# Dealing the staged Strassen products evenly over the steps of an MLP, and starting four output gates before the last products are transposed

## The chip, the core and the metric

The kernel runs on one core of a Trainium2 chip. The metric is device time in microseconds of one execution. The median of three runs before the change is 1495.2 us (1494.3 to 1498.37). Lower is better.

## The reference

One decoder layer over 256 tokens of width 2048, in float32. Cut to what this change touches:

```python
r = r + merged @ w_o[i]                                        # attention and convolution branches, ahead of it
h = rms_norm(r, g_mlp[i])
r = r + jnp.square(jax.nn.relu(h @ w_up[i])) @ w_down[i]       # 2048 -> 8192 -> 2048
h = rms_norm(r, g_ple[i])
r = r + jax.nn.sigmoid(h @ w_ple_gate[i]) * (p[i] @ w_ple_proj[i])   # 2048 -> 2048, and 256 -> 2048
```

## The kernel before

Everything is held transposed: features on the 128 partitions, the 256 tokens along the row. A float32 number is split into a rounded high part and a low rest (`w_hi`/`w_lo`, and for activations the two halves of an `x` tile), and a product is built from high*high, high*low and low*high. ScalarE (ACT) makes the high part, VectorE (DVE) the low one. A **unit** is one 128-column slice of a weight matrix, 128x2048 numbers: `cols` runs 32 matmuls for it, 16 of 512 columns (weights high, both parts of the activation) and 16 of 256 columns (weights low). It writes one PSUM bank, `ps_up` for a slice of w_up, `ps_dn` for one of w_down, `ps_pg` for one of w_ple_gate.

The MLP is 96 **steps** g = 0..95, one unit each: four quarters, each of about 16 up units (`ps_up`) and then 8 down units (`ps_dn`). The down units cover output columns 8 to 15 of w_down (in slices of 128) for the 16 up results of their quarter. Output columns 0 to 7 are computed another way: seven products P1 to P7 (`P`, one PSUM bank each, Strassen's scheme on 2x2 blocks) accumulate over 32 pairs j of up results. Each pair goes through four **stages** x = 0..3, which load nothing new but make the high and low parts that the products read:

- x = 0: the sums `s_raw` of the up results, then `s` high and low, and `b_hi`/`b_lo` (B11 and B22);
- x = 1: `t` (T1 and T3), then `t_hi`/`t_lo`;
- x = 2: `t` (T2 and T4), and `b` high and low (B21);
- x = 3: `t_hi`/`t_lo` of these, and ahead of them the four `s_raw` sums of the next pair, if its up results are there.

The matmuls that belong to a stage (6, 6, 3 and 6 of 512 columns, `products`) stand one step later on TensorE, behind that step's unit. How many stages a step takes is a table worked out in front of the loop (`staged`, from `quota`).

From g = 2 on, each engine's instructions keep the order in which the program gives them (`ordered`). A step g gives: the load of unit g+3 (`load_raw`) and of the pair that is staged two steps later (`load_pair`); the unit's matmuls; the split of the first half of unit g+2 (`w_hi`, `w_lo`); the work on the results of the unit before (`up_sum`, `up_high`, `up_low`, or `dn_done`); the stages; the split of the second half of unit g+2; the copy of the unit's PSUM bank to SBUF on ACT (`evacuated`: tiles `up` or `dn`); the products. There is a single bank for the units of the MLP ([7], the other seven hold P1 to P7), so unit g+1 starts on TensorE only when ACT has copied unit g's bank, and that copy stands on ACT behind the stages and the second `w_hi` of its step. The `hi` and `lo` tiles are 7 each, shared by units and stages; the `raw` tiles that the loads fill are 4; other tiles of 2 KB a row come from 45 slots.

The residual waits in DRAM (`r_kept`). In the first three quarters `dn_done` adds a down result to it with two accumulating DMAs on the POOL queue, one for each half of the tile `dn`, into the same place. At g = 85 all eight 256-row pieces are loaded into tiles `r`. In the last quarter `dn_done` adds on DVE instead (`r<-dn`), and after every second unit calls `enter_ple`: the squares of the piece are added to `ss2` (`sq`, `ss`), and two `x` tiles (`hP`) are made for the output gates.

When the last stage's products have run, `end_products` combines P1 to P7 on DVE (`u2`, `c11`, `u3`, `c21`, `c12`, `c22`), and four groups of four 128x128 transposes (`tr`) bring the result into the layout of `r`, where DVE adds it (`end_r`, `r<-tr`) and `enter_ple` follows. Then sixteen output gates run (`ps_pg`, each with a small `ps_proj`); the first needs all sixteen `hP` tiles.

Of the kernel before, what the change touches and what calls it, by code (L numbers as in the profile page):

```python
# [8 lines left out]
F32 = mybir.dt.float32  # L9
# [7 lines left out]
P = 128  # L17
S = 256
# [18 lines left out]
def hybrid_block_kernel(ctx: ExitStack, tc: tile.TileContext, ins: dict, out: bass.AP):  # L37
# [18 lines left out]
    def slot(shape, dtype, name):  # L56
        return bp.tile(shape, dtype, tag="slot", name=name)
# [24 lines left out]
    def load(*args):  # L82
        return inorder(nc.sync.dma_start(*args))
# [392 lines left out]
    up_at = {i: g for g, (kind, i) in enumerate(units) if kind == "up"}  # L476
    NU = len(units)

    todo = [(j, x) for j in range(32) for x in range(4)]
    staged = []  # L480
    for g in range(NU + 1):
        kind = units[min(g, NU - 1)][0]
        quota = (2 if g >= 72 and g % 2 == 0 else 1) if kind == "up" else 3 if g >= 88 or g % 4 == 0 else 2
        some = []
        while todo and len(some) < quota and up_at[2 * todo[0][0] + 1] + 3 <= g:
            some.append(todo.pop(0))
        staged.append(some)
    assert not todo

    def stages(g):  # L490
        return staged[g] if 0 <= g < len(staged) else ()

    def load_raw(g):
        if g < NU:
            kind, i = units[g]
            w = ins["w_up"][i] if kind == "up" else ins["w_down"][16 * i[0] + i[1]]
            wU[g] = [wp.tile([P, UNIT], F32, tag="raw", name="raw", bufs=4)]
            load(wU[g][0], w)

    def half_tiles(name):  # L500
        return tuple(wp.tile([P, HALF], F32R, tag=t, name=f"{name}_{t}") for t in ("hi", "lo"))

    def unit_half(g, h):

        if g >= NU:
            return (lambda: None,) * 2
        raw = wU[g][0][:, h * HALF:(h + 1) * HALF]
        hi, lo = half_tiles("w")
        wU[g].append((hi, lo))
        return lambda: high(hi, raw), lambda: low(lo, raw, hi)  # L510
# [102 lines left out]
    def enter_ple(u):  # L613
        square_sum(ss2, len(hP), r[u])
        for i in range(2):
            xsplit(hP, 2 * u + i, r[u][:, i, :], col(G_PLE + 2 * u + i))

    def dn_done(q, n, st):
        if q < 3:
            for i in range(2):  # L620
                nc.gpsimd.dma_start(r_kept[n // 2][:, n % 2, :], st[:, i * S:(i + 1) * S], accum_op=ALU.add)
# [10 lines left out]
    def end_products():  # L632
# [11 lines left out]
        for n, m in ((0, (c11, c21)), (2, (c11, c21)), (4, (c12, c22)), (6, (c12, c22))):  # L644
            pending.append(lambda n=n, m=m: transposed(n, m, end_r))

    for g in range(2):
        load_raw(g)
        for h in range(2):
            for work in unit_half(g, h):  # L650
                work()
    load_raw(2)
    ended = False
    for g in range(NU):
        kind, i = units[g]
        ordered[0] = g > 1
        if g == 3:
            banks["acc"] = [7]
        load_raw(g + 3)
        for j, x in stages(g + 2):  # L660
            if x == 0:
                load_pair(j)
        if g == 85:
            for u in range(8):
                r[u] = slot([P, 2, S], F32, f"r_{u}")
                nc.gpsimd.dma_start(r[u], r_kept[u])
        xs = hT if kind == "up" else {k: uT[16 * i[0] + k] for k in range(16)}
        ps = cols(wU[g][1:], xs, f"{kind}_{g}")
        if g == 0:
            rstd1 = rstd_columns(ss1, "mlp")  # L670
        if g == 1:
            row1 = rstd_rows(rstd1, "mlp")
        done = [n for n in range(g) if n in evac] if g > 1 else []
        ups = [units[n][1] for n in done if units[n][0] == "up"]
        on_act, on_dve = unit_half(g + 2, 0)
        on_act()
        for n in done:
            if units[n][0] == "up":
                up_sum(units[n][1], evac.pop(n))
        on_dve()  # L680
        for k in ups:
            up_high(k)
        for k in ups:
            up_low(k)
        for n in done:
            if units[n][0] == "dn":
                dn_done(*units[n][1], evac.pop(n))
        for j, x in stages(g):
            for _, work in stage(j, x):
                work()  # L690
        for work in unit_half(g + 2, 1):
            work()
        evac[g] = evacuated(ps, kind)
        if kind == "up" and i == 63:
            up_sum(i, evac.pop(g))
            up_high(i)
            up_low(i)
        for j, x in stages(g - 1):
            products(j, x)
        if not ended and prod and not any(staged[g:]):  # L700
            ended = True
            end_products()
        run_pending(1)
    ordered[0] = False
    dn_done(3, 15, evac.pop(NU - 1))
    run_pending(len(pending))
    banks["acc"], banks["tr"] = [1, 2, 3, 4, 5, 7], [0, 6]


    praw = slot([P, 2, S], F32, "p")  # L710
# [19 lines left out]

    ready = []
    for n in range(16):
        wt = load_unit(ins["w_ple_gate"][n])
        if n % 4 == 0:
            wproj = load_half(ins["w_ple_proj"][n // 4])
        gate = cols(wt, hP, f"pg_{n}", flush=12)
        if n < 15:
            proj = cols([wproj], pT, f"proj_{n}", at=2 * (n % 4), nk=2)
        else:
            proj = bank("ps_proj_15")  # L740
            for k in range(2):
# [69 lines left out]
```

## Time and profile before

| | |
|---|---|
| median of three runs | 1495.2 us (1494.3 to 1498.37) |
| the profiled execution, its own time | 1497.43 us |
| its span, first to last instruction | 1495.7 us |
| TensorE busy (matmul / weight load) | 1452.7 us (97%) / 1239.2 us (83%) |
| VectorE, ScalarE, GpSimd busy | 1050.5 us (70%), 822.8 us (55%), 61.1 us (4%) |
| granted TensorE clock, mean | 0.992 |
| DMA | 288.89 MB, mean 193 GB/s |

Busy time of TensorE is that of modelled, overlapping matmuls, so 97% does not say that 97% of the span is at full pace: a matmul that runs at half clock is busy too. What an idle stretch of another engine costs is read from whether TensorE waits for it. Line 80 of the kernel is the helper that issues all matmuls, line 77 that of ACT, line 87 that of DVE, line 83 that of the loads, so the profile's rows are told apart by their tiles.

### The profile page before, as it was taken

Reading aid. Unit: us, or ns where it says so; the run is one execution under the profiler, and the core shown is the slowest. Engines: PE = TensorE matmul, PEld = TensorE weight load, DVE = VectorE, ACT = ScalarE, POOL = GpSimd, SP = SyncE. Lnnn points to the kernel's source line nnn. Section 1 sums busy time; section 2 is a strip of 40 time slices with the busy share of each in tenths; the row PEclk is TensorE's granted clock in tenths of the full one; section 3 lists DMA queues with packets and bytes.
Section 4 is the critical chain, followed back from the end, with each engine's and each line's share of the span. In section 5 each row is a group of like instructions: output and inputs, shape, how many; then the busy total and the mean of one; then the engine's idle time right before and its main releaser. Section 6 shows DMA issues by size and latency. Waiting matters only on the chain.

```text
span 1495.7 us, 19751 instructions
## 1 busy us (share of the span) xinstructions
PE 1452.7 (97%) x7528; PEld 1239.2 (83%) x7528; DVE 1050.5 (70%) x1547; ACT 822.8 (55%) x1280; POOL 61.1 (4%) x91
## 2 busy tenths in 40 slices
PE   8999999999999999999999999999999999988998
PEld 7888888888888888888887888788887878766887
DVE  7555677746455557668887688777887778876875
ACT  7655555454444445446665566555665556644543
POOL 0100000000000000000011000110001101000000
PEclk9999999999999999999999999999999999998999
DMA  9655445555655566554668565776557847544461
GB/s 340 223 171 189 172 173 169 179 194 190 197 192 189 185 250 205 205 182 169 217 188 233 180 206 188 199 209 193 215 169 199 252 157 258 165 151 155 161 216 39
DMA packets 133902, 288.89 MB, mean 193 GB/s; under 512 B 7600, under 2 KB 81584, under 8 KB 111792
## 3 DMA queue, kind: packets, MB, share of 16 engines
q1 hardware_dynamic: 125472, 277.11, 54.9%
q0 software_dynamic: 8192, 10.49, 4.2%
q8 instruction: 59, 0.97, 0.3%
q14 instruction: 35, 0.29, 0.1%
q10 hardware_dynamic: 144, 0.04, 0.0%
HBM read 277.12 MB, written 10.49 MB: 192 GB/s over the span
## 4 chain that ended last, share of the span: by engine, by line
PE 93%; DVE 2%; ACT 2%; issue 1%; DMA 1%; SPq 0%; ACTq 0%; DVEq 0%
PE ps_up L80 23%; PE ps_g L80 12%; PE ps_dn L80 11%; PE ps_conv L80 9%; PE P L80 9%; PE ps_o L80 6%; PE ps_y L80 6%; PE ps_pg L80 6%; PE ps_q L80 3%; PE ps_k L80 3%; PE ps_v L80 3%; ACT w_hi L77 1%; PE ps_proj L80 1%; DMA raw<-in_w_down_dram 1%; DVE t L87 1%
## 5 line engine op out<-in xcount | busy, mean ns | idle before, releaser
L87 DVE TENSOR_TENSOR w_lo<-raw,w_hi 128x1024 fp32r<-128x1024 f32 (+1 forms) x556 | 559.2, 1023 | 273.9 <-ACT w_hi L77 178.3
L77 ACT ACTIVATE w_hi<-raw 128x1024 fp32r<-128x1024 f32 (+1 forms) x556 | 486.4, 893 | 274.2 <-PE ps_g L80 66.7
L80 PE MATMUL ps_up<-x,w_hi 128*128 128x512 f32 x1024 | 257.8, 394 | 8.5 <-ACT up L77 8.5
L80 PEld LDWEIGHTS ps_up<-x,w_hi 128*128 128x128 f32 x1024 | 191.9, 189 | 52.9 <-ACT up L77 16.1
L80 PE MATMUL ps_g<-w_hi,x 128*128 128x512 f32 x512 | 159.1, 390 | 0.0
L80 PE MATMUL ps_dn<-x,w_hi 128*128 128x512 f32 x512 | 137.9, 415 | 19.8 <-ACT dn L77 19.8
L80 PEld LDWEIGHTS ps_dn<-x,w_hi 128*128 128x128 f32 x512 | 101.6, 201 | 45.8 <-ACT dn L77 25.4
L80 PEld LDWEIGHTS ps_up<-x,w_lo 128*128 128x128 f32 x1024 | 131.3, 191 | 5.0
L80 PE MATMUL ps_up<-x,w_lo 128*128 128x256 f32 x1024 | 132.8, 283 | 0.0
L77 ACT ACTIVATE t_hi<-t 128x1024 fp32r<-128x1024 f32 x64 | 67.6, 1056 | 109.9 <-DVE t L87 102.3
L80 PEld LDWEIGHTS ps_g<-w_hi,x 128*128 128x128 f32 x512 | 96.1, 188 | 19.8
L87 DVE TENSOR_TENSOR t_lo<-t,t_hi 128x1024 fp32r<-128x1024 f32 x64 | 78.3, 1223 | 44.8 <-ACT t_hi L77 31.3
L77 ACT ACTIVATE up<-ps_up 128x512 f32<-128x512 f32 x64 | 38.1, 595 | 119.2 <-PE ps_up L80 116.2
L80 PE MATMUL ps_g<-w_lo,x 128*128 128x512 f32 x256 | 99.6, 389 | 0.0
L80 PE MATMUL ps_conv<-x,w_hi 128*128 128x512 f32 x384 | 97.6, 397 | 0.0
L80 PEld LDWEIGHTS ps_conv<-x,w_hi 128*128 128x128 f32 x384 | 70.8, 188 | 13.3
L80 PE MATMUL ps_y<-w_hi,x 128*128 128x512 f32 x256 | 79.5, 389 | 0.0
L80 PE MATMUL P<-t_hi,s 128*128 128x512 f32 x192 | 70.2, 393 | 0.0
L80 PEld LDWEIGHTS ps_dn<-x,w_lo 128*128 128x128 f32 x512 | 65.6, 191 | 2.5
L80 PE MATMUL ps_dn<-x,w_lo 128*128 128x256 f32 x512 | 66.4, 283 | 0.0
L80 PE MATMUL ps_pg<-x,w_hi 128*128 128x512 f32 x256 | 64.7, 393 | 1.7 <-DVE x L87 1.7
L87 DVE TENSOR_TENSOR a<-up 128x256 f32<-128x256 f32 x64 | 27.1, 423 | 51.6 <-ACT up L77 51.6
(196 smaller groups left out, 2064.5 us busy)
## 6 DMA issues: line engine op xcount, KB each, us to landing
raw<-in_w_up_dram SPq DMA_DIRECT2D x64, 1024.0 KB, 5.1
raw<-in_w_in_dram SPq DMA_DIRECT2D x56, 1024.0 KB, 5.0
raw_s<-in_w_down_dram SPq DMA_DIRECT2D x128, 256.0 KB, 4.4
raw<-in_w_down_dram SPq DMA_DIRECT2D x32, 1024.0 KB, 5.4
raw<-in_w_qkv_dram SPq DMA_DIRECT2D x20, 1024.0 KB, 4.9
raw<-in_w_branch_dram SPq DMA_DIRECT2D x16, 1024.0 KB, 5.1
raw<-in_w_o_dram SPq DMA_DIRECT2D x16, 1024.0 KB, 4.9
raw<-in_w_ple_gate_dram SPq DMA_DIRECT2D x16, 1024.0 KB, 5.1
```

The source lines that it names most:

```text
L77: return inorder(nc.scalar.activation(*args, **kw))
L80: return inorder(nc.tensor.matmul(*args, **kw))
L87: return lambda *args, **kw: inorder(getattr(nc.vector, name)(*args, **kw))
```

## The change

**The table of stages.** Before, a down step takes 2 stages, every fourth one 3, and from step 88 on 3; an up step takes 1, and from step 72 on every second one 2. Now every down step takes 2, and an up step 1, and from step 76 on every second one 2. Stages per step:

| steps | before | now |
|---|---|---|
| 17 to 24 (down) | 2 2 2 3 2 2 2 3 | 2 2 2 2 2 2 2 2 |
| 25 to 28 (up) | 1 0 0 1 | 1 1 1 1 |
| 41 to 48, 49 to 52 | the same as 17 to 28 | the same as 17 to 28 |
| 65 to 72 (down) | 2 2 2 3 2 2 2 3 | 2 2 2 2 2 2 2 2 |
| 73 to 76 (up) | 1 0 0 2 | 1 1 1 2 |
| 77 to 87 (up) | 1 2 1 2 1 2 1 2 1 2 1 | the same |
| 88 to 95 (down) | 3 3 3 3 2 0 0 0 | 2 2 2 2 2 2 2 0 |

The last products so stand behind the unit of step 95, no longer of step 93. On DVE, in the last quarter, a step of before that takes three stages (x = 0, 1, 2 of a pair; `w_lo x2` is the second half of one unit and the first of the next):

```order
L87 TENSOR_TENSOR w_lo<-raw,w_hi 128x1024 x2
L87 TENSOR_TENSOR r_11340<-dn,r_11340 128x256 x2
L87 SCALAR_TENSOR_TENSOR x<-r_11340,vec,x 128x256 x2
L87 TENSOR_TENSOR b_lo<-raw_s,b_hi 128x1024
L87 TENSOR_TENSOR s_11791<-s_raw,s_11790 128x512
L87 TENSOR_TENSOR t_11796<-raw_s 128x1024
L87 TENSOR_TENSOR t_lo<-t_11796,t_hi 128x1024
L87 TENSOR_TENSOR t_11802<-raw_s,t_11796 128x512
L87 TENSOR_TENSOR t_11802<-t_11802,raw_s 128x512
L87 TENSOR_TENSOR b_1_11804<-raw_s,b_0_11803 128x512
```

and the step that takes the same pair's x = 0 and 1 now:

```order
L87 TENSOR_TENSOR w_lo<-raw,w_hi 128x1024 x2
L87 TENSOR_TENSOR b_lo<-raw_s,b_hi 128x1024
L87 TENSOR_TENSOR s_11833<-s_raw,s_11832 128x512
L87 TENSOR_TENSOR t_11838<-raw_s 128x1024
L87 TENSOR_TENSOR t_lo<-t_11838,t_hi 128x1024
```

The three instructions of x = 2 have moved to the next step, and the residual's additions and `x` tiles have left this one.

**The residual in the last quarter.** `dn_done` adds on DVE only for n = 12 to 15; n = 8 to 11 go to `r_kept` by accumulating DMAs, as in the quarters before. The pieces 0 to 3, 6 and 7 are loaded at g = 85, piece 4 at 92, piece 5 at 94, and `enter_ple` runs for piece 4 in step 94, 5 and 6 in step 95, 7 in step 96. The end of the POOL queue, before:

```order
L666 DMA r_11340<-r_kept_4627 128x512
L666 DMA r_11342<-r_kept_4628 128x512
L666 DMA r_11344<-r_kept_4629 128x512
L666 DMA r_11346<-r_kept_4630 128x512
L113 TENSOR_TENSOR rstd_ple<-rstd_ple,half 128x2
```

and now:

```order
L670 DMA r_11342<-r_kept_4630 128x512
L644 DMA r_kept_4627<-dn 128x256 x4
L644 DMA r_kept_4628<-dn 128x256 x2
L670 DMA r_11861<-r_kept_4627 128x512
L644 DMA r_kept_4628<-dn 128x256 x2
L670 DMA r_12010<-r_kept_4628 128x512
L113 TENSOR_TENSOR rstd_ple<-rstd_ple,half 128x2
```

Eight accumulations were put in, and the loads of pieces 4 and 5 stand behind those that they depend on.

**Halves of gates.** Two more steps, 96 and 97, take the second halves (k = 8 to 15) of the weights of gates 0, 1 and 2, 3. Their matmuls run into the banks of P2, P6, P4 and P5 once these are read; the first halves (k = 0 to 7) follow behind the loop, into the same banks. TensorE behind the last products, before (gate tiles are those of `ps_pg`; 12069 to 12208 are the four groups of transposes):

```order
L406 MATMUL tr_12069<-ident,c_12057 128x128
L406 MATMUL tr_12130<-ident,c_12057 128x128
L406 MATMUL tr_12069<-ident,c_12060 128x128
L406 MATMUL tr_12069<-ident,c_12057 128x128
L406 MATMUL tr_12069<-ident,c_12060 128x128
L80 MATMUL ps_dn_12084<-x,w_hi 128x512 x15
L80 MATMUL ps_dn_12084<-x,w_lo 128x256 x16
L80 MATMUL ps_dn_12084<-x,w_hi 128x512
L406 MATMUL tr_12130<-ident,c_12060 128x128
L406 MATMUL tr_12130<-ident,c_12057 128x128
L406 MATMUL tr_12130<-ident,c_12060 128x128
L80 MATMUL ps_dn_12145<-x,w_hi 128x512 x15
```

and now (12200, 12217, 12249 and 12266 are gates 0 to 3):

```order
L406 MATMUL tr_12174<-ident,c_12165 128x128
L406 MATMUL tr_12174<-ident,c_12162 128x128
L406 MATMUL tr_12174<-ident,c_12165 128x128
L80 MATMUL ps_pg_12200<-x,w_hi 128x512 x6
L406 MATMUL tr_12234<-ident,c_12165 128x128
L406 MATMUL tr_12234<-ident,c_12162 128x128
L406 MATMUL tr_12234<-ident,c_12165 128x128
L80 MATMUL ps_pg_12249<-x,w_hi 128x512 x6
L406 MATMUL tr_12283<-ident,c_12164 128x128
L406 MATMUL tr_12283<-ident,c_12166 128x128
L406 MATMUL tr_12283<-ident,c_12164 128x128
L406 MATMUL tr_12283<-ident,c_12166 128x128
```

The two down units between the transposes are gone from there, and six matmuls of gate 0 and six of gate 2 stand in their places; the rest of the four halves (gate 0: 10, gate 1: 16, gate 2: 10, gate 3: 16 matmuls) stands between the third and the fourth group of transposes.

The diff, cut to its core:

```diff
+    units += [("pg", (0, 1)), ("pg", (2, 3))]
+    gates = {}
...
-        quota = (2 if g >= 72 and g % 2 == 0 else 1) if kind == "up" else 3 if g >= 88 or g % 4 == 0 else 2
+        quota = 2 if kind == "dn" or g >= 76 and g % 2 == 0 else 1
...
+    def load_halves(raw, gates, h):
+        for i, n in enumerate(gates):
+            load(raw[:, i * HALF:(i + 1) * HALF], ins["w_ple_gate"][n][:, h * HALF:(h + 1) * HALF])
+
+    def gate_part(n, wt, ks, first):
+        ps = gates[n]
+        def high_part(k):
+            mm(ps, wt[0][:, k % 8 * P:(k % 8 + 1) * P], hP[k].rearrange("p a s -> p (a s)"), start=first and k == ks[0], stop=not first and k == ks[-1])
+        for k in ks if first else ks[:-1]:
+            high_part(k)
+        for k in ks:
+            mm(ps[:, S:], wt[1][:, k % 8 * P:(k % 8 + 1) * P], hP[k][:, 0, :], start=False, stop=False)
+        if not first:
+            high_part(ks[-1])
...
     def dn_done(q, n, st):
-        if q < 3:
+        if q < 3 or n < 12:
...
         else:
             add_to_r(n, st)
-            if n % 2 == 1:
-                enter_ple(n // 2)
...
         if g == 85:
-            for u in range(8):
-                r[u] = slot([P, 2, S], F32, f"r_{u}")
-                nc.gpsimd.dma_start(r[u], r_kept[u])
+            for u in (0, 1, 2, 3, 6, 7):
+                load_r(u)
+        if g in (92, 94):
+            load_r(g // 2 - 42)
+        if kind == "pg":
+            banks["acc"] = [1, 5, 3, 4] if i[0] == 0 else [3, 4, 2, 7]
...
+        for u in {94: (4,), 95: (5, 6), 96: (7,)}.get(g, ()):
+            enter_ple(u)
+        if kind == "pg":
+            for n, wt in zip(i, wU[g][1:]):
+                gates[n] = bank(f"ps_pg_{n}")
+                gate_part(n, wt, range(8, 16), True)
...
-    banks["acc"], banks["tr"] = [1, 2, 3, 4, 5, 7], [0, 6]
+    banks["acc"] = [2, 7, 1, 5, 3, 4]
...
-        gate = cols(wt, hP, f"pg_{n}", flush=12)
+        if n < 4:
+            gate = gates[n]
+            gate_part(n, split_half(raw[:, n % 2 * HALF:(n % 2 + 1) * HALF]), range(8), False)
+        else:
+            gate = cols(wt, hP, f"pg_{n}")
```

More of the change, by code (lines that the diff above doesn't have):

```diff
@@ L491, in stages @@
         return staged[g] if 0 <= g < len(staged) else ()
+    def load_halves(raw, gates, h):
[11 more added lines that the diff above has]
+            high_part(ks[-1])
     def load_raw(g):
-        if g < NU:
+        if g < len(units):
             kind, i = units[g]
-            w = ins["w_up"][i] if kind == "up" else ins["w_down"][16 * i[0] + i[1]]
             wU[g] = [wp.tile([P, UNIT], F32, tag="raw", name="raw", bufs=4)]
-            load(wU[g][0], w)
+            if kind == "pg":
+                load_halves(wU[g][0], i, 1)
+            else:
+                load(wU[g][0], ins["w_up"][i] if kind == "up" else ins["w_down"][16 * i[0] + i[1]])
     def half_tiles(name):
@@ L503, in unit_half @@
     def unit_half(g, h):
-        if g >= NU:
+        if g >= len(units):
             return (lambda: None,) * 2
@@ L645, in end_products, with load_r @@
             pending.append(lambda n=n, m=m: transposed(n, m, end_r))
+    def load_r(u):
+        r[u] = slot([P, 2, S], F32, f"r_{u}")
+        nc.gpsimd.dma_start(r[u], r_kept[u])
     for g in range(2):
@@ L653, in hybrid_block_kernel @@
     ended = False
-    for g in range(NU):
+    for g in range(len(units)):
         kind, i = units[g]
@@ L663, in hybrid_block_kernel @@
         if g == 85:
-            for u in range(8):
-                r[u] = slot([P, 2, S], F32, f"r_{u}")
-                nc.gpsimd.dma_start(r[u], r_kept[u])
-        xs = hT if kind == "up" else {k: uT[16 * i[0] + k] for k in range(16)}
-        ps = cols(wU[g][1:], xs, f"{kind}_{g}")
+            for u in (0, 1, 2, 3, 6, 7):
[4 more added lines that the diff above has]
+            banks["acc"] = [1, 5, 3, 4] if i[0] == 0 else [3, 4, 2, 7]
+        else:
+            xs = hT if kind == "up" else {k: uT[16 * i[0] + k] for k in range(16)}
+            ps = cols(wU[g][1:], xs, f"{kind}_{g}")
         if g == 0:
@@ L687, in hybrid_block_kernel @@
                 dn_done(*units[n][1], evac.pop(n))
+        for u in {94: (4,), 95: (5, 6), 96: (7,)}.get(g, ()):
+            enter_ple(u)
+        if kind == "pg":
+            for n, wt in zip(i, wU[g][1:]):
+                gates[n] = bank(f"ps_pg_{n}")
+                gate_part(n, wt, range(8, 16), True)
         for j, x in stages(g):
@@ L692, in hybrid_block_kernel @@
             work()
-        evac[g] = evacuated(ps, kind)
+        if kind != "pg":
+            evac[g] = evacuated(ps, kind)
         if kind == "up" and i == 63:
@@ L704, in hybrid_block_kernel @@
     ordered[0] = False
-    dn_done(3, 15, evac.pop(NU - 1))
     run_pending(len(pending))
-    banks["acc"], banks["tr"] = [1, 2, 3, 4, 5, 7], [0, 6]
+    banks["acc"] = [2, 7, 1, 5, 3, 4]
     praw = slot([P, 2, S], F32, "p")
@@ L732, in hybrid_block_kernel @@
     for n in range(16):
-        wt = load_unit(ins["w_ple_gate"][n])
+        if n >= 4:
+            wt = load_unit(ins["w_ple_gate"][n])
+        elif n % 2 == 0:
+            raw = wp.tile([P, UNIT], F32, tag="raw", name="raw", bufs=4)
+            load_halves(raw, (n, n + 1), 0)
         if n % 4 == 0:
             wproj = load_half(ins["w_ple_proj"][n // 4])
-        gate = cols(wt, hP, f"pg_{n}", flush=12)
+        if n < 4:
+            gate = gates[n]
+            gate_part(n, split_half(raw[:, n % 2 * HALF:(n % 2 + 1) * HALF]), range(8), False)
+        else:
+            gate = cols(wt, hP, f"pg_{n}")
         if n < 15:
```

## The prediction

> **What bounds the kernel now.** I read the page's busy times first, then who waits for whom on TensorE, then the busy times by stage, and last the chain of waits and the instructions in order of time inside the stages that lose time.
>
> ```profile
> span 1495.7 us, 19751 instructions
> PE 1452.7 (97%) x7528; PEld 1239.2 (83%) x7528; DVE 1050.5 (70%) x1547; ACT 822.8 (55%) x1280; POOL 61.1 (4%) x91
> ...
> PE ps_dn L80 <- ACT dn L77: 19.8, 8, 3.4
> PE ps_up L80 <- ACT up L77: 8.5, 10, 3.0
> ```
>
> TensorE is the bound, and its longest waits, 28.3 us, are for ACT's copy of the one bank of the MLP's units. The change removes no matmul, so it can only win back waits and their clock. The busy times by stretch show where these are (quarters 1 to 3 from the first down unit to the fourth up unit behind them, in the third to the fifth; the up steps 78 to 87; the down units 88 to 93; from there to gate 4):
>
> ```profile
> core 0: us, PE busy (x) PEld busy (x) DVE busy (x) ACT busy (x) POOL busy (x), PEclk, DMA share, GB/s
> ...
> 758.30:859.68 101.38, 97.53 (x523) 83.38 (x522) 77.36 (x101) 57.22 (x74) 13.67 (x16) 1.00 0.72 207
> 936.06:1038.98 102.92, 99.08 (x523) 84.54 (x522) 77.36 (x101) 57.21 (x74) 13.68 (x16) 0.98 0.71 204
> 1115.35:1224.71 109.36, 103.18 (x535) 87.83 (x534) 82.41 (x108) 60.29 (x80) 13.65 (x16) 0.97 0.71 205
> 1224.71:1299.63 74.92, 74.22 (x400) 63.61 (x399) 63.84 (x95) 46.84 (x66) 4.40 (x8) 1.00 0.63 206
> 1299.63:1367.09 67.46, 55.04 (x263) 45.36 (x262) 49.49 (x70) 32.66 (x43) 0.00 (x0) 0.92 0.47 158
> 1367.09:1415.74 48.65, 44.45 (x244) 37.39 (x244) 39.68 (x70) 27.95 (x49) 0.72 (x1) 0.96 0.47 162
> ```
>
> What these would take without a wait follows from the chain of waits, where it runs along TensorE undisturbed, and around step 44, where it leaves it:
>
> ```profile
> 936.06 5.55 PE ps_dn L80 x32
> ...
> 956.14 2.74 PE P L80 x12
> 958.88 3.67 PE ps_dn L80 x18
> ...
> 963.33 1.23 DVE b_lo L87
> 964.55 0.60 DVE s L87
> 965.15 1.15 DVE t L87
> ...
> 967.37 1.04 ACT w_hi L77
> 968.40 0.49 ACT dn L77
> ...
> 968.94 7.43 PE ps_dn L80 x32
> ```
>
> A unit takes 5.55 us, a product matmul 2.74 / 12 = 0.228. At g = 44 a third stage puts b_lo, s and t in front of ACT's `t_hi`, `w_hi` and copy; TensorE's own work (5.55 + nine products, 2.06) ends at 966.49, it starts again at 968.94, and then runs the unit in 7.43 us, at a lowered clock. Each stretch of the table, less this work (the table's counts have one or two matmuls that only cross its ends):
>
> - quarters 1 and 2: 13 units and 105 products, 96.1 us; lost 5.3 and 6.8
> - quarter 3: 13 units and 117 products, 98.8; lost 10.5
> - steps 78 to 87: 10 units and 78 products, 73.3; lost 1.6
> - down units 88 to 93: 6 units and 69 products, 49.0; lost 18.4.
>
> That is 42.6 us, and the tail's loss comes below.
>
> **The change part by part. Durations on DVE,** from step 76 (x = 0 and 1 beside an up result; the last row is TensorE's next unit in the chain of waits):
>
> ```profile
> 1208.07 0.29 DVE L87 TENSOR_TENSOR s_raw<-a 128x128 f32<-128x128 f32 x1
> ...
> 1209.00 1.22 DVE L87 TENSOR_TENSOR b_lo<-raw_s,b_hi 128x1024 fp32r<-128x1024 f32 x1
> 1210.13 0.69 DVE L87 TENSOR_TENSOR s<-s_raw,s 128x512 fp32r<-128x512 f32 x1
> 1210.73 1.22 DVE L87 TENSOR_TENSOR t<-raw_s 128x1024 f32<-128x1024 f32 x1
> 1213.08 1.23 DVE L87 TENSOR_TENSOR t_lo<-t,t_hi 128x1024 fp32r<-128x1024 f32 x1 [1.12 <-ACT t_hi L77]
> ...
> 1214.53 7.45 PE ps_up L80 x32
> ```
>
> From start to start DVE takes 1.13 us for 1024 columns, 0.6 for 512 and 0.93 for the four s_raw; these are the durations used throughout.
>
> **Quarters 1 to 3.** Steps with two stages already stand there: the one at 936.06 and the two behind it ran without a gap, with 5.55 us a unit and 6, 9 and 12 products between them. All eight down steps now have 9 or 12 products behind them (6 behind the first). ACT's second `w_hi` and copy take 1.04 + 0.49 behind a unit's end, under the 2.06 that nine products cover. DVE's work in the longer of the two kinds of step (x = 1 and 2) is two w_lo, t and t_lo at 1.13 us from start to start, three of 512 columns at 0.6, and the wait of 1.1 to 1.2 us for `t_hi`: 7.5 us, beside 8.3 us of TensorE (5.55 + 12 products). I count 0.1 to 0.2 us for eight such steps. The two empty up steps, in which no product covers the copy (8.5 us of such waits in 10), get 6 and 3 products; 3 products are 0.69 us, about the copy's time, for 0.2 to 0.3. So quarters 1 and 2 fall to 96.5 us each, from 101.4 and 102.9: **-4.9 and -6.4**. In quarter 3 step 76 stays tight, the one ahead of 1214.53. TensorE waited 3.0 there (the longest `up` wait above) and lost 7.45 - 5.55 = 1.9 on the clock behind it. Now six products stand in that wait (1.37), and the four s_raw are made a step earlier, in the stage x = 3 that has moved to step 75. That leaves 3.0 - 1.4 - 0.9, about 0.7 to 1, and I count no lowered clock behind it. Loss 1.6 in all, 100.4 us: **-9.0**.
>
> **The last quarter's down units.** Eight units and 69 products ahead of the last nine are 44.4 + 15.7 = 60.1 us. The stages stand in the other phase here (x = 2, 3 in one step, 0, 1 in the next). The dearer one, x = 0 and 1, costs DVE two w_lo, b_lo, t and t_lo at 1.13, s at 0.6 and the 1.2 us for `t_hi`: 7.4 us, beside 7.6 of TensorE; its partner 6.2 beside 8.3. For n = 8 to 11 the two additions (0.88 us a unit) leave DVE; for n = 12 to 14 they remain and meet step 93, which I count at 8.2 against 7.6. I take 1.5 us of loss for all eight, nearer to the quiet steps of the quarters before (0.1 each) than to the three-stage ones of this quarter (18.4 / 6 = 3.1 each), since no step has a third stage. 61.6 us from 1299.63.
>
> The eight accumulations go to POOL, whose queue is one behind the other (the last row is a weight load in the first quarter, the slowest that the chain of waits has there):
>
> ```profile
> POOL r_kept L621 <- DMA r_kept<-dn: 108.0, 24, 8.6
> ...
> r_kept<-dn POOLq DMA_DIRECT2D x48, 128.0 KB, 3.9
> ...
> r<-r_kept POOLq DMA_DIRECT2D x8, 256.0 KB, 6.0
> ...
> 768.69 0.85 POOL L621 DMA_DIRECT2D r_kept<-dn  x1 [2.97 <-DMA r_kept<-dn]
> ...
> 780.48 8.79 DMA raw<-in_w_down_dram
> ```
>
> A pair takes 108.0 / 24 + 0.85 = 5.35 us from its first issue to its second on the mean and 9.5 at worst, beside a step of 8. Piece 5's load then starts 10 us behind the copy of unit 91 (5.35, then 3.9 to landing, and the issue) and lands 6 us later, two steps on; ACT wants it one step after that, in step 95. I cost it at nothing, with one step as cover; were the pairs at their worst, it would come up to 6 us late. SP issues eight half loads of gates for four whole ones, four more issues; its queue waits on free tiles through all these steps.
>
> **The tail.** Before, from the end of unit 93 (1367.09) to gate 4:
>
> ```profile
> 1361.98 0.88 DVE L87 TENSOR_TENSOR r<-dn,r 128x256 f32<-128x256 f32 x2
> ...
> 1368.57 0.69 DVE L87 TENSOR_TENSOR u<-P,p 128x512 f32<-128x512 f32 x1 [1.36 <-PE P L80]
> ...
> 1373.90 0.69 DVE L87 TENSOR_TENSOR r<-tr,r 128x512 f32<-128x512 f32 x1
> ...
> 1376.90 0.61 ACT L77 ACTIVATE sq<-r 128x512 f32<-128x512 f32 x1
> 1377.42 0.89 ACT L77 ACTIVATE x<-r,vec 128x256 fp32r<-128x256 f32 x2
> ...
> 1379.97 0.33 PE tr L406 x3
> ...
> 1397.89 0.70 PE ps_proj L80 x4
> 1398.59 0.79 PE ps_ss_ple L80 x8
> ...
> 1404.17 0.43 PE ps_rstd_ple L80 x2
> ```
>
> Its work is nine products 2.05, two down units 11.1, sixteen transposes 1.7, four gates 22.2, four proj 2.8, ss and rstd 1.2: 41.1 of 48.65 us; it lost 7.6. Now the two down units stand ahead of it, and 30.0 us of work remain. Counted from the end of unit 95: one w_lo stands ahead of u on DVE, so u starts at 2.15, c21 ends at 5.8 (u, c11, u3 at 0.6, a w_lo 1.13, c21), the other three combinations at 7.6, the first r<-tr at 8.2, a w_lo at 9.3, then ss and two x for piece 0 (10.7), the last dn added (11.5), ACT's square and x (1.1) and DVE's two x: 13.4. Until then TensorE can do the products, twelve transposes (1.3) and the twelve gate matmuls that stand between them (2.6), 6.0 us; the rest of the halves stands behind gate 0's k = 14, which needs that x. So 7.4 us are lost, then 24.0 of work remain. With 1.1 for a lowered clock (once 1.7 or not at all) and for the first proj, which needs the load of p: **38.5 us**, lower end 30.0, upper end 42 (two lowered clocks, 3.4).
>
> **The sum.** Before 101.4 + 102.9 + 109.4 + 74.9 + 67.5 + 48.65 = 504.7. Now 96.5 + 96.5 + 100.4 + 74.9 + 61.6 + 38.5 = 468.4. Difference 36.3. The profiled execution took 1497.4 (span 1495.7) and lies 0.15% above the median of 1495.2; 1495.2 - 36.3 = **1459 us**. Nearly all of it comes from the table of stages; the tail loses as much as before.
>
> [...] The gap of 2.45 us ahead of 968.94 was followed by a unit at a lowered clock, 7.43 us for 5.55. [...]
>
> **The rivals.** (a) *Two stages are still too many in the last quarter.* For it: its step x = 0, 1 has 0.2 us of room, and w_hi waits for free tiles. Against it: the same seven tiles serve the quiet steps. Four such steps with the gap and clock of g = 44 (2.46 + 1.9) make 17 us less gain: 1476. (b) *The halves cover the tail.* If gate 0's k = 14 came by the time TensorE reaches it, the tail were 33 us and the time 1453; against it, the chain of DVE above has no slack. (c) *Slower: the accumulations hold up the end.* Piece 5 is queued behind eight accumulations and ACT behind piece 5 (its squares stand ahead of the last copies). It decides from where a pair takes so long that the 36 us are gone: four pairs, 6 us late at 9.5 each, so 9.5 + 30/4, about 17 us a pair, three times the mean: 1500 or more. [...] (d) *The deal changes nothing, since another wait ends last at the same time* (the raw loads: the 8.79 us of the row above are more than a step). Then quarters 1 to 3 keep their loss, 1479.
>
> **How the numbers follow.** The forecast (1450 to 1468) has 0.66, (a) or (d) in part or whole (1468 to 1482) 0.18, (b) 0.08, (c) 0.03; 0.05 is left for a wait that I don't see, half of it within 0.3% and half slower. A measurement here can tell about 0.3% (4.5 us) from no change. The hard floor is all the loss gone: 42.6 + 7.6, 1445. The range 1449 to 1476 leaves out (c), the end of (a) and (d), and the floor. Faster 0.66 + 0.18 + 0.08 = 0.92, same 0.03, slower 0.05.
>
> **What would show it.** Right: ACT's copies of `dn` no longer make TensorE wait in steps 17 to 24 and their like; the first three quarters' stretches at 96 to 101 us; the granted clock at 1.00 in them; down units 88 to 95 in 60 to 63; one wait of the transposes for c and one of `ps_pg` for x at the tail. Wrong: waits of ps_dn for ACT in the last quarter (a); ACT's `sq` waiting for r<-r_kept (c).

## The result, and the profile after

The changed kernel takes 1460.92 us (median of four runs, 1460.54 to 1460.98), beside 1496.5 for the kernel before on the same chip: ratio 0.9762, 95% interval 0.9745 to 0.9779. The forecast was 1459, in a range of 1449 to 1476. The profiled execution took 1460.54 us, with a span of 1458.7.

The head of the page, and the list of who makes TensorE wait (in total, how often, the longest), after:

```profile
span 1458.7 us, 19769 instructions
PE 1439.8 (99%) x7528; PEld 1232.5 (84%) x7528; DVE 1046.6 (72%) x1539; ACT 823.4 (56%) x1280; POOL 68.1 (5%) x99
...
PE tr L406 <- DVE c L87: 3.1, 2, 1.7
PE ps_up L80 <- ACT up L77: 2.8, 4, 1.1
PE ps_pg L80 <- DVE x L87: 1.9, 1, 1.9
PE ps_dn L80 <- ACT dn L77: 0.6, 1, 0.6
```

The two waits for ACT's copy were 19.8 and 8.5 us and are 0.6 and 2.8. DVE and ACT are as busy as before: no work went away, it only stands elsewhere. The busy times by stretch, cut at the same places as before, with the tail in the last row (length, then the busy times of PE, PEld, DVE, ACT and POOL, the granted clock, the DMA share, GB/s):

```profile
757.53:854.12 96.59, 96.59 (x522) 83.59 (x521) 77.87 (x102) 57.51 (x74) 13.75 (x16) 1.00 0.76 217
930.52:1027.11 96.59, 96.59 (x522) 83.60 (x521) 77.86 (x102) 57.62 (x74) 13.63 (x16) 1.00 0.76 217
1103.50:1204.27 100.77, 99.65 (x534) 85.77 (x533) 82.40 (x108) 60.32 (x80) 13.61 (x16) 1.00 0.76 215
1204.27:1278.76 74.49, 74.23 (x400) 63.62 (x398) 63.88 (x94) 47.00 (x66) 3.32 (x6) 1.00 0.62 211
1278.76:1340.15 61.39, 60.83 (x326) 52.09 (x325) 52.05 (x72) 38.13 (x51) 8.04 (x10) 1.00 0.76 223
1340.15:1378.90 38.75, 33.42 (x180) 27.66 (x179) 32.49 (x56) 22.22 (x41) 0.72 (x1) 0.96 0.47 170
```

In quarters 1 and 2 TensorE is busy for the whole of the stretch, at full clock. The chain of waits there, at the place of step 44, where it had left TensorE for DVE and ACT, is now unit, products, unit, with nothing between:

```profile
953.50 5.55 PE ps_dn L80 x32
959.05 2.06 PE P L80 x9
961.11 5.59 PE ps_dn L80 x32
```

The tail, from the end of unit 95 (1340.15) on, TensorE first, and then the splits (w_lo) that stand on DVE among the sums and x tiles (start, duration, and in brackets the idle time ahead and who ended it):

```profile
1344.04 0.30 PE L406 MATMUL tr<-ident,c 128*128 128x128 f32 x1 [1.66 <-DVE c L87]
...
1346.27 0.55 PE L406 MATMUL tr<-ident,c 128*128 128x128 f32 x3 [1.40 <-DVE c L87]
1346.57 2.51 PE L80 MATMUL ps_pg<-x,w_hi 128*128 128x512 f32 x6
...
1353.83 0.90 PE L80 MATMUL ps_pg<-x,w_hi 128*128 128x512 f32 x2 [1.88 <-DVE x L87]
```

```profile
1340.33 2.36 DVE L87 TENSOR_TENSOR w_lo<-raw,w_hi 128x1024 fp32r<-128x1024 f32 x2 [0.26 <-ACT w_hi L77]
1344.40 1.22 DVE L87 TENSOR_TENSOR w_lo<-raw,w_hi 128x1024 fp32r<-128x1024 f32 x1
1348.53 1.22 DVE L87 TENSOR_TENSOR w_lo<-raw,w_hi 128x1024 fp32r<-128x1024 f32 x1
```

A wait of 3.3 us in three pieces, after which six matmuls of gate 0 take 2.3 us, with a granted clock of 0.50 from 1347.04 to 1350.45, where 1.37 would do (six of 0.228); then 1.88 us for the x tile of k = 14.

### The profile page after: what moved, and what is told of

It reads as the page before. It is cut to its first block, busy times and chain, and to the rows that moved or that the text cites. A ratio compares the mean times of both kernels' runs of the same rounds, so it can differ in the third digit from the quotient of the medians.

```text
span 1458.7 us, 19769 instructions
## 1 busy us (share of the span) xinstructions
PE 1439.8 (99%) x7528; PEld 1232.5 (84%) x7528; DVE 1046.6 (72%) x1539; ACT 823.4 (56%) x1280; POOL 68.1 (5%) x99
## 4 chain that ended last, share of the span: by engine, by line
PE 95%; DVE 2%; ACT 1%; issue 1%; DMA 0%; DVEq 0%; ACTq 0%
PE ps_up L80 24%; PE ps_g L80 12%; PE ps_dn L80 11%; PE P L80 10%; PE ps_conv L80 9%; PE ps_o L80 6%; PE ps_y L80 6%; PE ps_pg L80 6%; PE ps_q L80 3%; PE ps_k L80 3%; PE ps_v L80 3%; PE ps_proj L80 1%; ACT w_hi L77 1%; DVE w_lo L87 1%; PE ps_s L80 0%
## 5 line engine op out<-in xcount | busy, mean ns | idle before, releaser
L80 PEld LDWEIGHTS ps_up<-x,w_hi 128*128 128x128 f32 x1024 | 191.0, 188 | 46.8 <-ACT up L77 10.2
L80 PE MATMUL ps_dn<-x,w_hi 128*128 128x512 f32 x512 | 127.4, 391 | 0.6 <-ACT dn L77 0.6
L80 PEld LDWEIGHTS ps_dn<-x,w_hi 128*128 128x128 f32 x512 | 96.0, 188 | 20.5 <-ACT dn L77 1.5
L80 PEld LDWEIGHTS ps_g<-w_hi,x 128*128 128x128 f32 x512 | 96.1, 188 | 19.8
L644 POOL DMA_DIRECT2D r_kept<-dn x56 | 47.9, 908 | 556.0 <-ACT dn L77 398.4
```

What stands on the lines that cost most here:

```text
L80: return inorder(nc.tensor.matmul(*args, **kw))
```

## The experiments

The profiled executions are compared by two lengths, each from starts of units in the trace: **early**, the sum of units 17 to 30, 41 to 54 and 65 to 78, and **late**, from the start of unit 88 to the last matmul. Medians are of 4 or 5 runs; the kernel before stood at 1493.95 to 1498.13 on three chips, and on each chip its executions spread by 5 to 11 us, those of the other kernels by 3 or less. So the ratios carry the spread of the kernel before, and differences of a few us are read from the lengths. A length is that of one execution; the two traces of the changed kernel agree in both within 0.3 us.

| kernel | median us | ratio to before (95%) | early | late |
|---|---|---|---|---|
| before | 1493.95 to 1498.13 | | 316.4 | 191.2 |
| changed | 1460.92 | 0.9762 (0.9745 to 0.9779) | 296.7 | 175.3 |
| new table for steps 17 to 87 alone | 1476.65 | 0.9872 (0.9842 to 0.9903) | 296.5 | 191.1 |
| changed, old table for steps 17 to 87 | 1481.26 | 0.9902 (0.9875 to 0.9929) | 316.5 | 176.8 |
| new table alone | 1466.53 | 0.9806 (0.9781 to 0.9832) | 296.5 | 180.4 |
| and later entries | 1464.38 | 0.9785 (0.9756 to 0.9814) | 296.7 | 178.0 |
| and accumulations (changed, no halves) | 1463.11 | 0.9792 (0.9779 to 0.9806) | 296.7 | 177.4 |
| changed, additions on DVE | 1462.88 | 0.9791 (0.9778 to 0.9805) | 296.7 | 176.1 |
| changed, threes at 18 and 22 | 1483.74 | 0.9919 (0.9893 to 0.9945) | 318.0 | 175.3 |
| changed, threes at 20 and 23 | 1464.51 | 0.9787 (0.9758 to 0.9816) | 300.0 | 175.3 |
| changed, tail pinned | 1463.6 | 0.9795 (0.9782 to 0.9809) | 296.7 | 179.4 |
| changed, tail filled | 1456.26 | 0.9746 (0.9733 to 0.976) | 296.7 | 170.8 |
| and eight banks | 1455.21 | 0.9721 (0.9692 to 0.975) | 296.7 | 170.0 |
| changed, again | 1461.68 | 0.9766 (0.9737 to 0.9795) | 296.5 | 175.2 |

**1. The table for steps 17 to 87, alone.** In the kernel before:

```diff
-        quota = (2 if g >= 72 and g % 2 == 0 else 1) if kind == "up" else 3 if g >= 88 or g % 4 == 0 else 2
+        quota = 2 if kind == "dn" or g >= 76 and g % 2 == 0 else 1
+        quota += g >= 88
```

> The kernel before, with the new table of stages for steps 17 to 87 alone (the last quarter's down steps stay at 3 3 3 3 2 0 0 0, no accumulations there, no halves of gates). Theory, the gain comes from the table, step by step: the three stretches from a quarter's first down unit to the fourth up unit behind it fall to 96.6, 96.6 and 100.8 us, as in the changed kernel, from 101.4, 102.9 and 109.4, and nothing else moves: 1496.5 - 19.7 = 1476.8, between 1474 and 1479. Rival, the halves of gates and the accumulations free engines and carry the gain: no change, 1494 to 1498.

1476.65; the early length fell by 20.0 us and the late one stayed. What is left of TensorE's waits for the copy of `dn` belongs to the last quarter:

```profile
PE ps_dn L80 <- ACT dn L77: 12.4, 5, 3.4
```

So these 20 us need nothing of the rest of the change.

**2. The mirror image:** the changed kernel with the old line, its `g >= 88 or g % 4 == 0` turned into `g < 88 and g % 4 == 0`.

> The changed kernel with the old table for steps 17 to 87 (2 2 2 3 2 2 2 3, then 1 0 0 1), the rest as changed. Theory: the mirror image of the run before, 1460.9 + 19.7 = 1480.6, between 1478 and 1483; in the trace a gap of about 2.5 us on TensorE behind the fourth down step of each quarter, and 0.7 ahead of two up units. Rival, the parts of the change need each other (loads or tiles freed by one serve the other): the sum of this run's loss and the last one's gain differs from each other by more than 4 us.

1481.26, early 19.7 us longer. The two runs give 20.0 and 19.7: in the early length the table and the rest of the change add up. The late length of this run is 1.5 us above that of the changed kernel, with a wait of 3.5 us for an x tile in the tail (1.9 in the changed kernel).

**3. The whole new table and nothing else** (the line of the change in the kernel before).

> The kernel before with the whole new table and nothing else: the residual is added on VectorE in the last quarter, the gates run whole behind the transposes. Theory: the down units gain as in the changed kernel, less 1 to 3 us for the additions; the tail has no gate halves to run while the sums and transposes go on, so it waits until the last x of the four transposed groups: they take 2.2 us each on VectorE behind 6 to 8 us of sums, so some 18 to 20 us behind unit 95 instead of 13.7, with 25 us of TensorE's work left. 44 to 46 for the tail instead of 38.8, and 1467 to 1471 in all, middle 1469. Rival, the halves carry the last quarter's gain: about 1477, as with the early table alone.

1466.53, just under the expected range, but not for the reason given. The two rows are the units 88 to 95 by their starts, and unit 95 to the last matmul:

```profile
1279.88:1339.76 59.88, 56.44 (x295) 46.93 (x293) 51.20 (x77) 35.30 (x49) 0.00 (x0) 1.00 0.53 174
1339.76:1460.30 120.54, 115.07 (x646) 100.04 (x644) 89.03 (x146) 58.12 (x101) 0.72 (x1) 0.97 0.44 151
```

and of the changed kernel:

```profile
1278.76:1334.61 55.85, 55.29 (x295) 47.17 (x294) 46.64 (x63) 33.97 (x44) 8.04 (x10) 1.00 0.77 223
1334.61:1454.07 119.46, 114.13 (x646) 98.88 (x644) 89.98 (x152) 60.27 (x106) 0.72 (x1) 0.99 0.43 148
```

The down units lose 4.0 us without the rest of the change, not 1 to 3, and the tail only 1.1, not 5 to 7: while VectorE made the x tiles, TensorE did 17 matmuls of gate 0 between its waits. So a part of the gain sits in the down units and is not the table. The next three runs find it.

**4. The entries later, the additions still on VectorE** (run 3, and):

```diff
             add_to_r(n, st)
-            if n % 2 == 1:
-                enter_ple(n // 2)
...
+        for u in {94: (4,), 95: (5, 6)}.get(g, ()):
+            enter_ple(u)
...
     dn_done(3, 15, evac.pop(NU - 1))
+    enter_ple(7)
```

> The run of before with the new table alone, with one more edit: the squares and x tiles of pieces 4 to 7 are made in steps 94, 95 and behind the loop, as in the changed kernel, instead of behind every second unit; the residual is still added on VectorE, the gates run whole. The units 88 to 95 started 59.9 us apart with the table alone, 56.7 with the changed kernel's later entries but additions on VectorE, 55.9 with the change whole. Theory, the place of these entries is worth about 3 us and the accumulating DMAs about 1: 56.7 for the stretch, 1463.5 in all (1462 to 1465). Rival, the accumulations and the later entries only pay together, since either alone leaves VectorE behind: 59 to 60 and 1466 to 1467.

The stretch is the 56.7 us that was expected, and the median, 1464.38, lies in the expected range:

```profile
1279.84:1336.52 56.68, 55.42 (x294) 47.09 (x293) 49.76 (x73) 34.33 (x46) 0.00 (x0) 1.00 0.58 194
```

**5. No halves:** the changed kernel without the steps 96 and 97; gates 0 to 3 as before.

> The changed kernel without the two steps of gate halves: gates 0 to 3 run whole behind the transposes, as before. With the table alone (the run of before with the new table) the stretch from the start of unit 95 to the last matmul was 120.5 us, against 119.5 in the changed kernel, so theory: the halves are worth 1 to 2 us, 1462.5 in all (1461 to 1464). Rival, they carry what the table does not: the table alone stands at 1466.5, and this run comes out there, 1465 to 1468.

**6. Additions on VectorE in the changed kernel:**

```diff
-        if q < 3 or n < 12:
+        if q < 3:
...
-            for u in (0, 1, 2, 3, 6, 7):
+            for u in range(8):
                 load_r(u)
-        if g in (92, 94):
-            load_r(g // 2 - 42)
```

> The changed kernel with the residual of n = 8 to 11 added on VectorE instead of by accumulating DMAs; the squares and x tiles of pieces 4 to 7 stay where the change put them (steps 94 to 96), and all pieces are loaded at step 85. With the table alone the units from 88 to 95 started 59.9 us apart, 55.9 in the changed kernel. Theory, two additions a unit (0.88 us) put VectorE behind, and the squares and x tiles in steps 90 and 92 as much again: this run loses half of the 4.0 us, +1 to 3, so 1463. Rival one, the additions are all of it: 1465. Rival two, the squares and x tiles are all of it: 1461.

Both medians came out as expected, 1463.11 and 1462.88. The down units, first without halves, then with additions on VectorE:

```profile
1279.54:1335.74 56.20, 55.44 (x294) 47.15 (x293) 47.04 (x65) 34.55 (x46) 8.04 (x10) 1.00 0.78 223
```

```profile
1279.17:1335.86 56.69, 55.45 (x294) 47.08 (x293) 49.37 (x71) 33.73 (x44) 0.00 (x0) 1.00 0.58 191
```

Together the runs 3 to 6 are a ladder for the late length: 191.2 before, 180.4 with the table (-10.8), 178.0 with the later entries (-2.4; the down units gain 3.2 and the tail gives 0.8 back, since more is left for it), 177.4 with the accumulations (-0.6), 175.3 with the halves (-2.0). Runs 4 and 6 have additions on VectorE and late entries, and both have 56.7 for the down units; without these additions they are 0.5 (run 5) and 0.8 us (the changed kernel) shorter, not 2.0 as half of the 4.0 would be. Even that is not shown to be the accumulations': in runs 10 and 11, which have them too, the same stretch takes 56.6 and 57.1, and no run explains why. Squares and x tiles of four pieces cost more at their old place than eight additions, by the traces (3.2 us beside 0.5 to 0.8); the medians of 4, 5 and 6 (1464.4, 1463.1, 1462.9) lie too near each other to tell them apart.

**7. Is it three stages that a step can't hold?** The changed kernel, with 16 stages in a quarter's down steps dealt as 2 3 1 2 2 3 1 2:

> The changed kernel with 2 3 1 2 2 3 1 2 stages in the down steps of quarters 1 to 3 (16 as in its own 2 2 2 2 2 2 2 2; no empty up steps): the six steps of three take x = 2, 3 and the next pair's x = 0, the kind ahead of which the kernel before had its gaps of 2.46 us. Theory, a step with three stages is the dear one, and it costs 2.6 to 4.2 us (gap, and a lowered clock behind it in some): 1460.9 + 16 to 25, so 1477 to 1486, middle 1480. Rival one, it is dear only where DVE was already behind from the steps ahead of it, and a step of one stage behind it gives it back: 1461 to 1466. Rival two, the empty up steps carried the early gain: within 2 us of 1460.9.

**8. The same number of threes, elsewhere** (2 2 1 3 2 1 3 2):

> The changed kernel with 2 2 1 3 2 1 3 2 stages in the down steps of quarters 1 to 3: again six steps of three, none empty, but each behind a step of one stage, and of the kinds x = 1, 2, 3 and x = 3, 0, 1. With each ahead of a step of one stage (2 3 1 2 2 3 1 2, kind x = 2, 3, 0) they cost 2.5 us of gap each and 21.5 us in all. Theory one, three stages are more than one step holds, whatever stands ahead: 1478 to 1484. Theory two, what counts is what VectorE still owes from the step ahead; behind a step of one stage it starts 1 to 2 us earlier and the gaps shrink to under 1 us each: 1462 to 1468.

By their times run 7's theory (1477 to 1486) and run 8's theory two (1462 to 1468) came out: 1483.74 and 1464.51. But both texts misname the kinds. By the table of stages the steps 17 to 24 take (x of each step, of which 0 begins the next pair):

```
before              12  30   12  301  23  01  23   012
changed             12  30   12  30   12  30  12   30
2 3 1 2 2 3 1 2     12  301  2   30   12  301 2    30
2 2 1 3 2 1 3 2     12  30   1   230  12  3   012  30
```

The first cost 21 us of early length, 3.6 a step, the second 3.2 us in all. The chain of waits at step 18 of run 7, and after it ACT's row of that `t_hi`:

```profile
764.68 3.55 PE ps_dn L80 x17
768.22 1.14 DVE t_lo L87
769.36 1.14 DVE b_lo L87
770.50 0.60 DVE s L87
771.09 1.15 DVE t L87
...
773.29 1.04 ACT w_hi L77
774.33 0.49 ACT dn L77
...
774.86 5.84 PE ps_dn L80 x32
```

```profile
772.33 1.06 ACT L77 ACTIVATE t_hi<-t 128x1024 fp32r<-128x1024 f32 x1 [3.44 <-DVE t L87]
```

In a step 3, 0, 1 the `t` of x = 1 comes late on VectorE, behind t_lo, b_lo and s. ACT stands idle for 3.44 us for it, and ACT's copy of the unit's bank is queued behind the `t_hi` that it waits for. At steps 20 (2, 3, 0) and 23 (0, 1, 2) of run 8 the chain hardly leaves TensorE:

```profile
786.80 1.39 PE P L80 x6
...
788.49 5.84 PE ps_dn L80 x32
```

Here six products (the step ahead had one stage) cover the copy not quite, and the gap is 0.32 us. In the kernel before, step 24 (0, 1, 2, behind a step of two) has none: nine products, and at their end the next unit:

```profile
823.11 2.06 PE P L80 x9
825.17 5.57 PE ps_up L80 x32
```

So neither theory holds as it was put. A step of three is not dear by its number: step 24 has two stages ahead of it and costs nothing. What differs is when VectorE has the `t` behind which ACT's `t_hi`, `w_hi` and copy stand. First step 18 of run 7, then step 24 of before:

```profile
771.01 1.22 DVE L87 TENSOR_TENSOR t<-raw_s 128x1024 f32<-128x1024 f32 x1
```

```profile
820.49 1.22 DVE L87 TENSOR_TENSOR t<-raw_s 128x1024 f32<-128x1024 f32 x1
```

At step 18 `t` is ready at 772.23, 2.0 us behind the end of the step's unit (764.68 + 5.55): VectorE had not been idle from 763.73 on, and the four s_raw and t_lo of x = 3 stand ahead of b_lo, s and `t`. At step 24 `t` is ready at 821.71, 1.4 us ahead of the unit's end (823.11): VectorE had been idle for 0.51 and 0.20 us ahead of the two w_lo, and of the stages only b_lo and s stand ahead of `t`. ACT waits for `t` there too, for 2.57 us, but in time. How much of this is the kind of step and how much the work that the step ahead left over, these runs don't separate. In the last quarter of before, where four such steps stand in a row (2, 3, 0; 1, 2, 3; 0, 1, 2; 3, 0, 1) and the residual's additions and x tiles stand on VectorE too, every one of them is followed by a gap, of 2.0, 1.6, 2.4 and 3.4 us: there 0, 1, 2 is dear as well, so the kind alone does not decide either.

**9. The splits of the first halves kept out of VectorE's chain** (changed kernel; the four `split_half` of the first halves placed behind `run_pending(len(pending))`, ahead of `ordered[0] = False`):

> The changed kernel with one thing pinned: the splits of the first halves of gates 0 to 3 keep their place in program order, behind the last x tile of the four transposed groups, instead of standing on VectorE among the sums of the products (three w_lo of 1.13 us ahead of gate 0's k = 14). Theory, that matmul waits for VectorE's chain and starts 3 to 3.6 us earlier, 10 instead of 13.7 us behind the end of unit 95; some of it comes back as waits for these splits later: 1459, between 1457 and 1460. Rival, VectorE has as much work before gate 4 in any order, and TensorE waits the same time in another place: 1461, within 1 us.

Neither: 1463.6, slower (ratio 0.9795 for 0.9762). Gate 0's k = 14 started 11.7 us behind unit 95 instead of 13.7, but the late length grew by 4.1 us.

```profile
PE ps_pg L80 <- DVE x L87: 3.2, 1, 3.2
...
PE ps_ss_ple L80 <- DVE ss L87: 2.3, 1, 2.3
```

The edit keeps the fourth group of transposes in program order too; it stands on TensorE behind the halves, as in the changed kernel (1361.67, there 1362.51). So VectorE, with the splits pinned behind that group, idled for 4.44 us, and the four splits came after it:

```profile
1362.31 0.69 DVE L87 TENSOR_TENSOR r<-tr,r 128x512 f32<-128x512 f32 x1 [4.44 <-PE tr L406]
...
1366.23 4.63 DVE L87 TENSOR_TENSOR w_lo<-raw,w_hi 128x1024 fp32r<-128x1024 f32 x4
```

In the changed kernel VectorE makes four splits in that hole (1357.5 to 1364.0). TensorE's waits in the tail are 1.7 us longer in all than in the changed kernel, and its granted clock is 0.50 for 10.2 us of the tail, for 3.4 there (means over the two executions 0.996 and 0.998); 6.8 us more at half clock are an estimated 3.4 us of work, the larger of the two.

**10. TensorE's order in the tail written out.** `gate_hi(n, ks)` and `gate_lo(n, ks)` issue the matmuls of gate n with the high and the low weights of these k, `first_hi` and `first_lo` split its first half, and `run_pending(1)` gives one group of transposes with its r<-tr. Cut to its core:

```diff
+    banks["acc"] = [7, 5, 1, 3]
+    first_hi(0), first_hi(1)
+    dn_done(3, 15, evac.pop(NU - 1))
+    for n in range(4):
+        gate_hi(n, range(8, 14))
+        gate_lo(n, range(8, 14))
+        run_pending(1)
+        if n == 0:
+            enter_ple(7)
+        enter_ple(n)
+        if n == 2:
+            first_hi(2), first_lo(0)
+    for n in range(4):
+        gate_hi(n, (14, 15))
+        gate_lo(n, (14, 15))
+    first_lo(1), first_lo(2), first_hi(3), first_lo(3)
+    for n in range(2):
+        gate_hi(n, range(6))
+    ...
```

> The changed kernel with the tail written out by hand: behind the last products TensorE runs k = 8 to 13 (high and low) of gates 0, 1, 2, 3 in turn, with one group of transposes behind each, then k = 14 and 15 of all four, then the first halves; gate 0 goes into the bank of the MLP's units, which is free 1.6 us earlier than the sums of products; VectorE does all sums first, then the last residual addition, piece 7, and the groups, and the splits of the first halves last. Theory, the tail's 8.7 us of loss (waits of 3.3, 1.9 and less, and two stretches of lowered clock) are there only because nothing else stood in TensorE's order: 14 us of gate work now cover VectorE's 16 us, and 4 to 7 us come back: 1455.5, between 1453 and 1457. Rival, VectorE's chain to the last x tile is the bound of the tail: 1459 to 1461.

**11. And the banks of the transposes given on:** `banks["acc"] = [2, 4, 7, 5, 1, 3]` becomes `[2, 4, 0, 7, 5, 6, 1, 3]`.

> The kernel with the tail written out by hand, and the two banks of the transposes given to the projections and gates behind them too (eight banks in turn instead of six). In the run without them a gate still waited 1.6 us for VectorE to read the bank of an earlier projection, with a lowered clock in the gate behind. Theory, that wait goes and nothing takes its place: 1.5 to 2.5 us less, 1454.3 (1453 to 1456). Rival, the reads themselves are late because VectorE makes the splits of the next gates first, and the wait moves to the next reader: 1456.3, within 0.6.

**12. The changed kernel beside it:**

> The changed kernel once more, so that it stands beside the variants of its tail on one chip. Both theories: 0.9762 of the kernel before, 1458 to 1461.

Run 10 took 1456.26 and run 11 1455.21, both in the expected range; the changed kernel beside the latter took 1461.68 (1460.13 to 1462.78), 0.7 above its range, the filled tail 1453.5 to 1455.99, 6.5 us less by the medians and 5.3 by the late lengths. In the tails of runs 10 and 11 the granted clock is lowered nowhere up to the last matmul (means over the executions 0.999 and 1.000), and so not behind run 10's wait of 1.6 us, where run 11's text has it lowered; in the changed kernel's it is 0.50 for 3.4 us, in run 12's for 6.8 (0.998 and 0.997). Run 10 is several edits in one: it also loads the first halves and p in step 95 and reorders VectorE's work, and no run takes these apart from TensorE's order. TensorE's waits in run 11 (two of 0.2 us, one of them shown, are all that is left for its gates and transposes), and its two rows from unit 88 on:

```profile
PE ps_dn L80 <- ACT dn L77: 1.6, 2, 1.1
...
PE ps_pg L80 <- DVE o L87: 0.2, 1, 0.2
```

```profile
1278.80:1335.93 57.13, 55.49 (x294) 47.16 (x293) 47.10 (x63) 34.30 (x44) 8.03 (x10) 1.00 0.78 219
1335.93:1448.77 112.84, 112.29 (x646) 98.09 (x644) 88.41 (x152) 59.03 (x106) 0.72 (x1) 1.00 0.45 156
```

From the start of unit 95 the changed kernel took 119.46 us and this one 112.84, in which TensorE is busy for 112.29; the down units give 1.3 us back, in a wait for ACT of 1.1 us ahead of unit 94, which no run explains. Run 10 to run 11 is 1.05 us by the medians, of different chips, and 0.9 by the late lengths, with the wait of 1.6 us gone (0.2 now): less than the 1.5 to 2.5 expected. This is the fastest of the versions: 0.9721 of the kernel before.

## Why the prediction was right, and where it was not

| term | forecast us | measured |
|---|---|---|
| quarter 1 | 96.5 | 96.6 |
| quarter 2 | 96.5 | 96.6 |
| quarter 3 | 100.4 | 100.8 |
| steps 78 to 87 | 74.9 | 74.5 |
| eight down units and 69 products | 61.6 | 61.4 |
| tail to gate 4 | 38.5 | 38.75 |
| sum | 468.4 | 468.6 |

*Quarters 1 to 3* held, and runs 1 and 2 show that the table alone does it. Step 76 kept a gap of 1.12 us ahead of its next unit (forecast 0.7 to 1), with a granted clock of 1.00 behind it. *The mechanism* was named for step 44 as it is (b_lo, s and t ahead of `t_hi`, `w_hi` and the copy), but the working then counted by "a third stage", and run 8 and step 24 of before show that other steps of three cost a sixth of that or nothing. The term came out right because it was taken from the gaps themselves, and in each early quarter the gap stood behind the step of the kind 3, 0, 1.

*The last quarter* came out right in its sum, and its working named a wrong source. "Nearly all of it comes from the table of stages": by the lengths the table brings 20.0 us in the early part and 10.8 in the late one, 30.8 of some 36. The step that failed is the line on the down units, which priced what leaves VectorE as two additions of 0.88 us: the accumulations are worth 0.5 to 0.8 us there at most, and what mattered was moving the entries of pieces 4 and 5 out of the dense steps, 3.2 us in the units, of which the text said nothing but that they had moved. The halves, to which no gain of their own was given, bring 2.0. That the term of 61.6 us came out (61.4) is in part luck: its loss of 1.5 us was reckoned with the additions as the cost, and the place of the entries, worth more, was not reckoned at all.

*The tail's chain* stood as worked out, with a second w_lo ahead of u: u at 2.46 us for 2.15, k = 14 at 13.7 for 13.4. Ahead of it TensorE waited for 3.3 and 1.9 us, where the text has 7.4 lost. The 1.1 us in the sum for a lowered clock and the first proj was the author's estimate, and no run shows when a wait lowers the clock; here it was lowered once, to 0.50 for 3.41 us, an estimated 1.7 us of work. That it "has no slack" was a statement on VectorE's order as it is; run 10 shows that TensorE had 14 us of gate work for that time, in another order. Run 9 shows that taking the splits out of VectorE's chain does not gain by itself.

*The rivals.* (a) would have shown waits of ps_dn in the last quarter; there is one, 0.6 us. (b) needed gate 0's k = 14 by the time TensorE reaches it; it came 1.9 us later. (c): POOL's last rows in the last quarter:

```profile
1310.30 0.84 POOL L644 DMA_DIRECT2D r_kept<-dn  x1 [0.98 <-ACT dn L77]
1316.67 0.85 POOL L644 DMA_DIRECT2D r_kept<-dn  x1 [5.53 <-DMA r_kept<-dn]
1322.98 0.58 POOL L670 DMA_DIRECT2D r<-r_kept  x1 [5.46 <-DMA r_kept<-dn]
```

A pair took up to 6.4 us from issue to issue, and piece 5 was asked for 12.7 us behind its first accumulation (10 forecast), still 11.6 us ahead of step 95 (unit 95 starts at 1334.61). (d): the raw loads did not hold up quarters 1 and 2, which run without a gap at 217 GB/s (207 and 204 before).

## What to carry to other kernels

Where one engine's queue holds the instruction that frees another's bank, look at what stands ahead of it there and what that waits for: the same number of stages cost 3.6 us or nothing a step, depending on how late in the step VectorE made what an ACT instruction ahead of the copy waits for. When a stall at the end of a phase seems bound by one engine's chain, list what the stalled engine could already run and into which free bank; writing the tail out that way gave 5 to 6.5 us here, and keeping the splits out of the chain alone made it slower. And take a change of several parts apart even when its sum came out as forecast: 4 to 5 of 36 us came from the later entries and the halves, to which the working gave no gain.

## What the runs showed of the hardware

**The clock and gaps.** In the traces of the kernel before and of the changed one, between 700 us and the tail, ten gaps of 0.45 to 2.02 us stood ahead of a whole unit of 32 matmuls, and not one was followed by a lowered clock. Of seven gaps of 2.41 to 3.38 us, all in the kernel before, six were (7.2 to 7.5 us for the unit, beside 5.84 behind the gap of 2.02). Of its three gaps of 2.46 us, those ahead of units 45 and 69 were, and the one ahead of unit 21 was not (5.88 for the unit), so the length alone does not tell. In the kernel before the granted clock drops to 0.50 seven times between 25 us and the last matmul, each time for 3.41 us. In the 3.41 us from 789.35 on, across the gap ahead of unit 21, TensorE was idle for 1.8 us (3.41 less 1.58 busy), and the clock stayed at 1.00; in those from 966.85 on, across the gap ahead of unit 45, it was idle for 2.1 us (3.41 less 1.32), and then the clock was 0.50:

```profile
789.35:792.76 3.41, 1.58 (x7) 1.30 (x8) 2.36 (x2) 1.78 (x3) 1.69 (x2) 1.00 0.47 69
792.77:796.18 3.41, 3.41 (x22) 3.04 (x21) 0.21 (x1) 1.58 (x2) 0.81 (x1) 1.00 1.06 303
...
966.85:970.26 3.41, 1.32 (x6) 1.10 (x7) 2.36 (x2) 2.04 (x3) 0.85 (x1) 1.00 0.30 53
970.26:973.67 3.41, 3.41 (x10) 2.67 (x9) 0.00 (x0) 1.57 (x2) 0.59 (x1) 0.50 0.98 288
```

In the changed kernel's tail the wait of 3.3 us was followed by a drop (0.50 from 1347.04 to 1350.45), that of 1.9 was not (1.00 from 1353.86 to 1357.28). What decides it is not shown.

**The accumulating DMAs landed later with the new table.** With the old table 128 KB took a median of 3.9 us (3.7 in run 2) from issue to landing; with the new one, whether or not the last quarter has accumulations, 5.5 to 6.2 (the changed kernel twice, runs 1, 3, 5, 6 and 10), but 4.9 with the threes of run 7. It stayed hidden here, behind steps of 8 us. The cause is open. That the other transfers stand closer together (the DMA share of quarter 1 is 0.76 for 0.72) does not explain it by itself: from the start of unit 17 to that of unit 30 it is 0.70 in run 7 and 0.71 in the kernel before, and run 7's accumulations land 1.0 us later.
